# A four-layer hybrid trunk on one core: order of the start, width of v, place of o's transposes, and when norms and gates are issued

## The chip, the cores and the metric

One Trainium2 chip, of which the program uses one NeuronCore. The time is the device time of one execution in microseconds (us); the result compares medians of runs. The engines are PE (TensorE, matmuls and transposes by an identity), DVE (VectorE), ACT (ScalarE), POOL (GpSimd) and SP (SyncE, which here issues nearly all DMAs, one after the other in program order).

## The reference

The program computes four layers on x of 1024 positions by 1024 channels, all float32. Layers 0 and 3 are HGRN2, layer 1 is sliding-window attention, layer 2 is a gated DeltaNet:

```python
for i in range(4):
    shift, scale, gate = split(c @ ada_w[i] + ada_b[i], 3)      # 1024 each, from one vector c
    h = rmsnorm(x, norm_g[i]) * (1 + scale) + shift
    y = (hgrn2, swa, gdn)[i % 3](h, ...)                          # token mixer
    x = x + gate * y
# hgrn2: q, f, v, z = split(h @ w_in)  (8 heads of 128); per head a gated linear recurrence
#        S = f*S + k v^T, o = q S  (f = lb+(1-lb)*sigmoid(f_pre), k = (1-lb)*sigmoid(-f_pre))
#        y = (rmsnorm(o) * silu(z)) @ w_out
# swa:   16 query heads, 4 kv heads of 64, window 128, rotary angles from positions, sinks; gate silu(z)
# gdn:   q, k (8 heads), v, z (16 heads of 128), causal conv of 4 taps, silu, per-head decay,
#        delta rule with a triangular solve per chunk; y = (rmsnorm(o) * silu(z)) @ w_out
```

## The kernel before

**Precision and tiles.** Each float32 operand is split into a rounded high part and the rest, and each product is three matmuls (`mm3`, lines 204 to 206). Activations `hhi`, `hlo` lie with channels on partitions, in two halves of 512 positions (`hf` 0 and 1), 8 blocks (`k`) of 128 channels each. `load_w` (166) brings a weight tile of 256 KB by SP, ACT casts it to `w_hi` (179), DVE makes `w_lo` (180); four pairs are in flight. `proj_fm` gives 128 output channels by 512 positions (`proj_ps`, 24 matmuls of 512 columns per half). `proj_tm` (1170) gives positions by 256 channels (`projt_ps`, matmuls of 256 columns): v of HGRN for a pair of heads, and q, k, v of attention. `out_mm` (1204) is the output projection (`outp_ps`).

**Start.** `load_x` transposes x on PE and squares it on ACT. `ada_first` makes c @ ada_w in 512-wide parts, all four needed ones (2, 0, 3, 1, in that order, `AO`) as one-row matmuls on PE (400); `ada_cols` (449) turns a row into columns. Parts 2 and 0 hold the scale and shift of blocks 0 to 3, parts 3 and 1 those of blocks 4 to 7. `norm_apply` (496) conditions a half: per block one DVE product into `n_t`, one ACT instruction for `hhi` (505), one DVE instruction for `hlo` (506). The angle tables of attention (`rope_tables`) are made here too.

**Layers.** Each mixer is a generator. `weave` (68) steps several generators in the proportion of the costs that they yield: the mixing of unit or head n with the projections of n+1 and, as `side`, the ada matrices of the next layer on DVE (413). A list scheduler then orders the instructions of each engine by their place in the program, less the offset of `high_priority`; `early` (114) uses that for the first projections of a layer, and `tied` (138) holds a group of matmuls behind its first one.

**HGRN.** `mix` forms the causal products of each 128 positions by levels; the last (j = 32) takes three strips of 32 rows, of 96, 64 and 32 columns (1087). Then o per half (`o_ps`), its norm (1132), four transposes `ot_ps` (1136), the product with the gate z, and a store to the DRAM tile `od` by SP (1141), read back for the output projection. The last head stays on chip.

**DeltaNet.** `conv` copies a projection (644), scales it (648) and adds three shifted taps on DVE (650). `inverse` solves the triangular systems of a unit in small matmuls, the last of them four groups `z_ps`. `ZL` says in which unit the z of a later unit is projected, both halves (0, 1) at once mostly.

## Time and profile before

| | |
|---|---|
| median of 3 runs | 2692.0 us (2688.74 to 2692.27) |
| profiled execution | 2695.95 us, of which the span of the trace 2694.2 |
| PE busy | 2609.7 us, 97% of the span |
| DVE, ACT, POOL busy | 75%, 47%, 5% |
| layer 0, HGRN | 55 to 635 us |
| layer 3, HGRN | 2125 to 2694 us |

The profile is of one execution. "Busy" is the time in which an engine had an instruction at work; the wait rows give, for an engine's line, what it stood still for, the total, how often and the longest. PEclk is TensorE's granted clock as a share of full speed, in a window the mean over it.

### The profile page before, as it was taken

Reading aid. Unit: us, or ns where it says so; the run is one execution under the profiler, and the core shown is the slowest. Engines: PE = TensorE matmul, PEld = TensorE weight load, DVE = VectorE, ACT = ScalarE, POOL = GpSimd, SP = SyncE. Lnnn points to the kernel's source line nnn. Section 1 sums busy time; section 2 is a strip of 40 time slices with the busy share of each in tenths; the row PEclk is TensorE's granted clock in tenths of the full one; section 3 lists DMA queues with packets and bytes.
Section 4 is the critical chain, followed back from the end, with each engine's and each line's share of the span. In section 5 each row is a group of like instructions: output and inputs, shape, how many; then the busy total and the mean of one; then the engine's idle time right before and its main releaser. Section 6 shows DMA issues by size and latency. Waiting matters only on the chain.

```text
span 2694.2 us, 51458 instructions
## 1 busy us (share of the span) xinstructions
PE 2609.7 (97%) x18927; PEld 2102.4 (78%) x18927; DVE 2010.2 (75%) x5619; ACT 1272.9 (47%) x3268; POOL 136.7 (5%) x352
## 2 busy tenths in 40 slices
PE   8999999999999999999999999999999999999998
PEld 4878878778878777677877777777788878787877
DVE  6776766788687877777988888989876766656575
ACT  4333333444454655454556556666644433333342
POOL 0000100000000000001001101100000000000000
PEclk9999999999999999999999999999999999999999
DMA  6332222344223252333343333333584221111133
GB/s 241 92 93 84 68 79 72 110 137 157 59 87 103 75 158 91 114 98 84 102 115 99 96 105 100 94 97 82 179 254 132 71 60 37 56 51 43 49 118 115
DMA packets 361490, 273.29 MB, mean 101 GB/s; under 512 B 70499, under 2 KB 294166, under 8 KB 361238
## 3 DMA queue, kind: packets, MB, share of 16 engines
q1 hardware_dynamic: 360950, 268.96, 33.9%
q8 instruction: 149, 2.44, 0.4%
q14 instruction: 103, 0.84, 0.1%
q0 software_dynamic: 288, 1.05, 0.1%
HBM read 224.77 MB, written 45.15 MB: 100 GB/s over the span
## 4 chain that ended last, share of the span: by engine, by line
PE 71%; DVE 17%; DMA 5%; ACT 3%; issue 3%; SPq 1%; POOL 0%; DVEq 0%; ACTq 0%; POOLq 0%
PE proj_ps L206 10%; PE proj_ps L205 9%; PE proj_ps L204 9%; PE outp_ps L204 5%; PE outp_ps L205 5%; PE outp_ps L206 5%; DMA ada_w<-in_ada_w_dram 3%; PE projt_ps L204 3%; PE projt_ps L206 3%; PE projt_ps L205 3%; DVE w_lo L180 2%; DVE gd_tb L650 2%; PE pv_ps L1374 1%; DVE ada_acc L413 1%; PE w_ps L890 1%
## 5 line engine op out<-in xcount | busy, mean ns | idle before, releaser
L204 PE MATMUL proj_ps<-hhi,w_hi 128*128 128x512 f32 x1664 | 675.8, 406 | 6.1 <-ACT gd_tb L648 5.9
L206 PE MATMUL proj_ps<-hhi,w_lo 128*128 128x512 f32 x1664 | 679.9, 409 | 0.0
L205 PE MATMUL proj_ps<-hlo,w_hi 128*128 128x512 f32 x1664 | 671.2, 403 | 0.0
L204 PEld LDWEIGHTS proj_ps<-hhi,w_hi 128*128 128x128 f32 x1664 | 315.3, 190 | 59.4 <-ACT gd_tb L648 6.3
L205 PEld LDWEIGHTS proj_ps<-hlo,w_hi 128*128 128x128 f32 x1664 | 314.7, 189 | 59.0 <-issue 2.4
L206 PEld LDWEIGHTS proj_ps<-hhi,w_lo 128*128 128x128 f32 x1664 | 315.0, 189 | 56.1 <-issue 1.0
L179 ACT CAST w_hi<-w_raw 128x512 fp32r<-128x512 f32 x332 | 202.0, 611 | 303.3 <-PE proj_ps L205 188.1
L180 DVE TENSOR_TENSOR w_lo<-w_raw,w_hi 128x512 fp32r<-128x512 f32 x332 | 223.1, 674 | 155.2 <-ACT w_hi L179 129.1
L205 PE MATMUL projt_ps<-w_lo,hhi 128*128 128x256 f32 x896 | 258.7, 291 | 4.7 <-DVE w_lo L180 4.7
L204 PE MATMUL projt_ps<-w_hi,hhi 128*128 128x256 f32 x896 | 257.8, 290 | 0.6 <-ACT w_hi L179 0.6
L206 PE MATMUL projt_ps<-w_hi,hlo 128*128 128x256 f32 x896 | 256.8, 290 | 0.0
L204 PE MATMUL outp_ps<-o_hi,w_hi 128*128 128x512 f32 x576 | 229.2, 400 | 4.7 <-ACT o_hi L1200 3.4
L205 PE MATMUL outp_ps<-o_lo,w_hi 128*128 128x512 f32 x576 | 229.4, 399 | 0.0
L206 PE MATMUL outp_ps<-o_hi,w_lo 128*128 128x512 f32 x576 | 226.8, 396 | 0.7 <-DVE w_lo L183 0.7
L205 PEld LDWEIGHTS projt_ps<-w_lo,hhi 128*128 128x128 f32 x896 | 171.1, 192 | 8.1 <-DVE w_lo L180 6.0
L204 PEld LDWEIGHTS projt_ps<-w_hi,hhi 128*128 128x128 f32 x896 | 171.1, 192 | 3.7 <-ACT w_hi L179 1.0
L206 PEld LDWEIGHTS projt_ps<-w_hi,hlo 128*128 128x128 f32 x896 | 170.8, 192 | 2.4 <-issue 1.0
L650 DVE SCALAR_TENSOR_TENSOR gd_tb<-gd_xs,taps,gd_tb 128x512 f32<-128x512 f32 x192 | 145.2, 756 | 28.3 <-ACT gd_tb L648 19.7
L182 ACT ACTIVATE w_hi<-w_raw,par 128x512 fp32r<-128x512 f32 (+1 forms) x136 | 94.3, 698 | 137.0 <-PE outp_ps L205 89.2
L204 PEld LDWEIGHTS outp_ps<-o_hi,w_hi 128*128 128x128 f32 x576 | 108.8, 189 | 29.1 <-ACT o_hi L1200 4.9
L413 DVE SCALAR_TENSOR_TENSOR ada_acc<-ada_w,par,ada_acc 128x512 f32<-128x512 f32 x140 | 104.8, 749 | 33.4 <-DMA ada_w<-in_ada_w_dram 32.5
L206 PEld LDWEIGHTS outp_ps<-o_hi,w_lo 128*128 128x128 f32 x576 | 108.7, 189 | 23.5 <-DVE w_lo L183 1.3
(398 smaller groups left out, 4894.8 us busy)
## 6 DMA issues: line engine op xcount, KB each, us to landing
ada_w<-in_ada_w_dram SPq DMA_DIRECT2D x160, 256.0 KB, 2.8
w_raw<-in_hg_in_w_dram SPq DMA_DIRECT2D x136, 256.0 KB, 2.8
w_raw<-in_gd_in_w_dram SPq DMA_DIRECT2D x108, 256.0 KB, 3.0
o_in<-od SPq DMA_DIRECT2D x72, 256.0 KB, 3.2
w_raw<-in_gd_out_w_dram SPq DMA_DIRECT2D x64, 256.0 KB, 2.9
w_raw<-in_sw_in_w_dram SPq DMA_DIRECT2D x48, 256.0 KB, 2.9
w_raw<-in_hg_out_w_dram SPq DMA_DIRECT2D x40, 256.0 KB, 2.8
ada_w<-in_ada_w_dram SPq DMA_DIRECT2D x8, 1024.0 KB, 9.2
```

The costliest lines, as they stand in the source:

```text
L179: nc.scalar.copy(hi, raw)
L180: nc.vector.tensor_tensor(lo, raw, hi.bitcast(F32), ALU.subtract)
L182: nc.scalar.activation(hi, raw, AF.Copy, scale=scale)
L204: mm(out, a[0], b[0], start=start, stop=False)
L205: mm(out, a[0], b[1], start=False, stop=False)
L206: mm(out, a[1], b[0], start=False, stop=stop)
L413: self.nc.vector.scalar_tensor_tensor(acc, w, c, acc, ALU.mult, ALU.add)
L650: nc.vector.scalar_tensor_tensor(y, xs[:, j:j + HT], w(j), y, ALU.mult, ALU.add)
L890: nc.tensor.matmul(po[:, hd[a]], dd["u"][a, hf][:, cs], rhs, start=True, stop=True)
L1374: nc.tensor.matmul(po[a * 64:(a + 1) * 64], vg[:, n + 1 - nkb + b, :], p4[:, :, a, :], start=b == 0, stop=b == nkb - 1)
```

## The change

- **Start.** x's first half is fetched first and transposed, then ada parts 2 and 0 and two weight tiles each. `norm_apply` is a generator now: blocks 0 to 3 are made after parts 2 and 0, blocks 4 to 7 after parts 3 (PE) and 1 (DVE). x's later half comes after all of this; its transposes use the PSUM banks `tr` and `s`. The first projections get their places before the conditioning of the later half (`k.start`). The angle tables are made by the side stream of layer 0.
- **v of HGRN.** `load_wide` and `proj_wide` replace `proj_tm`: 512 channels at a time, four heads, evacuated into the slots of x, which is spilled to DRAM and filled again before the output projection. Spills and fills go by POOL's queue, those of layer 0's start by SP's.
- **o of HGRN, heads 0 to 6.** DVE writes the normed o in an order of 32-wide blocks, transposes it in 32 by 32 squares, and four DMAs store it into the DRAM tile `pd`; `gate()`, called at the third level of the next half, loads it, multiplies it by z, stores it to `od`.
- **Last level.** Four strips of 64, 64, 32 and 32 columns in place of three; the diagonal copies by ACT.
- **Norm's later half.** Before layer 2 its blocks are taken four at a time from within `conv` (`self.last`, `parts`, `hold`), and z of units 1 and 2 is projected early; `n_t` lies in PSUM. Before the other layers it is drained at the start of the mixer.
- **DeltaNet.** The four `z_ps` groups are held behind the last projection matmul (`apart`) and yield 2200; z of units 1 to 5 is projected by halves in two units.
- **Attention.** v and q first, k later, with one rsqrt per two blocks; the four pv matmuls in one group. Output: x is written from `hslot` tiles.

```diff
-NS = 8, 16, 10
...
-ZL = ((2, 0, 1),), ((3, 0, 1),), ((4, 0, 1),), ((5, 0, 1),), ((6, 0),), ((6, 1),), ((7, 0, 1),), ()
...
+ZL = ((2, 1), (3, 0)), ((3, 1), (4, 0)), ((4, 1), (5, 0)), ((5, 1),), ((6, 0),), ((6, 1),), ((7, 0, 1),), ()
...
+    def apart(self, mms):
+        with self.tc.issue_after(self.mm.ins):
+            self.tied(mms)
...
+    def load_wide(self, w, c0, pool):
+        return [self.load_w(w[:, k, c0:c0 + HT], None, (None, pool)[k % 2]) for k in range(KT)]
...
+                pt = self.psum(("tr", "s")[g], "x_ps", 1) if hf else self.proj_ps("x_ps")
...
+        for c in range(NC):
+            nc.scalar.activation(sq, xts[c], AF.Square, accum_out=ssq[:, c:c + 1])
...
+    def ada_load(self, i, part):
...
+        wk = self.hslot("ada_w0").bitcast(F32)
+        for g in range(2):
+            self.nc.sync.dma_start(wk[:, 4 * g:4 * g + 4, :], w[:, 4 * g:4 * g + 4, part * HT:(part + 1) * HT])
+        return wk
...
+    def ada_first(self, i, part, acc, wk, bank):
...
+        if bank:
+            pr = self.psum(*bank)
+            for k in range(KT):
+                nc.tensor.matmul(pr[0:1, :], self.cT[:, k:k + 1], wk[:, k, :], start=k == 0, stop=k == KT - 1)
...
+                self.ada_step(acc, wk[:, k, :], k)
+        self.ada_cols(i, part, acc)
...
-            t = self.np.tile([P, HT], F32, name="n_t", tag="n_t", bufs=NB["n_t"])
+            t = self.psum("lev", "n_t", 2)
...
-            nc.scalar.activation(hhi[:, k, :], t, AF.Identity, bias=S)
+            self.piece = nc.scalar.activation(hhi[:, k, :], t, AF.Identity, bias=S)
...
+            yield 1
...
-            nc.scalar.copy(xs[:, 3:], ps)
+            with self.tc.issue_after(self.hold.ins) if self.hold else nullcontext():
+                nc.scalar.copy(xs[:, 3:], ps)
...
-                nc.vector.scalar_tensor_tensor(y, xs[:, j:j + HT], w(j), y, ALU.mult, ALU.add)
...
+                last = nc.vector.scalar_tensor_tensor(y, xs[:, j:j + HT], w(j), y, ALU.mult, ALU.add)
+            self.piece = None
+            with self.tc.issue_after(last.ins):
+                drain(take(self.last, self.parts))
+            self.hold = self.piece
...
-            with self.burst():
...
+            self.apart([lambda g=g, z=z, p_=p_, b_=b_: nc.tensor.matmul(z[R[b_], g, :], uv[R[p_], g, R[b_]], Tc[R[p_], g, :], start=True, stop=True)
+                        for g in range(N) for z, p_, b_ in ((za, 0, 1), (zb, 2, 3))])
...
-            yield 900
+            yield 2200
...
-        self.early(proj_kq(0, ds[0], ((0,),)), EV)
+        self.parts = 4
+        self.early(chain(proj_kq(0, ds[0], ((0,),)), proj_z(1, ds[1], (0,)), proj_z(2, ds[2], (0,))), EV)
+        drain(self.last)
...
-        weave(self.tc, (inverse(0, ds[0]), 28000, 0, 0.8, 100),
-              (chain(proj_z(0, ds[0], (1,)), proj_v(0, ds[0]), proj_z(1, ds[1]), proj_kq(1, ds[1])), 72800, 0, 1, 0))
+        weave(self.tc, (inverse(0, ds[0]), 34300, 0, 0.85, 100),
+              (chain(proj_z(0, ds[0], (1,)), proj_v(0, ds[0]), proj_z(1, ds[1], (1,)), proj_kq(1, ds[1])), 62400, 0, 1, 0))
...
-            ws = self.load_tm(w_in, 2 * D + 2 * m * P)
...
+        def proj_v(m):
...
+            def ev(tt, ps):
+                hf, c = divmod(tt, NC)
+                if vs[hf] is None:
+                    vs[hf] = self.xslot("hg_v").rearrange("p (c a) n -> p c (a n)", a=2)
...
+                nc.scalar.copy(vs[hf][:, c, m * HT:m * HT + n], ps[:, :n])
...
+            yield from self.proj_wide(self.load_wide(w_in, 2 * D + m * HT, mp), ev, range(2 * NC))
...
+        def gate():
...
+            h, hf, z = pend.pop()
+            rows = (slice(h * P, (h + 1) * P), slice(hf * HT, (hf + 1) * HT))
+            t = tl("tmp")
+            nc.sync.dma_start(t, self.pd[rows])
+            nc.vector.tensor_tensor(v4(z, "c b"), v4(t, "b c"), v4(z, "c b"), ALU.mult)
+            nc.sync.dma_start(od[rows], z)
...
-                            nc.gpsimd.tensor_copy(at[gs, :, gs], A[gs].rearrange("p (c t) -> p c t", c=NC))
+                            nc.scalar.copy(at[gs, :, gs], A[gs].rearrange("p (c t) -> p c t", c=NC))
...
+                        def mm(c, k, g, x, b):
+                            return nc.tensor.matmul(pl[g * 32:(g + 1) * 32, c, b], kg[:, c * P + k * 32:c * P + (k + 1) * 32], xv[:, c, x, :], start=True, stop=True)
+                        self.tied([lambda c=c, m=m: mm(c, *m) for c in range(NC) for m in (
+                            (0, 3, slice(6, 7), slice(3, 4)), (0, 0, slice(0, 4, 3), slice(1, 3)),
+                            (1, 1, slice(1, 5, 3), slice(2, 4)), (2, 2, slice(2, 3), slice(3, 4)))])
+                        for k, g, b0, b1 in ((0, 0, 1, 3), (1, 1, 2, 4), (2, 2, 3, 4), (0, 3, 3, 4)):
+                            nc.scalar.copy(at[k * 32:(k + 1) * 32, :, b0 * 32:b1 * 32], pl[g * 32:(g + 1) * 32, :, b0:b1, :].rearrange("p c b t -> p c (b t)"))
                         yield 900
+                    if l == 3 and pend:
+                        gate()
...
-                nc.vector.tensor_tensor(on.rearrange("p (c t) -> p c t", c=NC), po.rearrange("p (c t) -> p c t", c=NC), r[:, :, None].to_broadcast([P, NC, P]), ALU.mult)
-                pt = self.psum("tr", "ot_ps", 1)
...
-                    nc.tensor.transpose(pt[:, cs], on[:, cs], self.ident)
...
-                nc.vector.tensor_tensor(of, pt, d["zs", hf], ALU.mult)
                 if h < HA:
-                    nc.sync.dma_start(od[h * P:(h + 1) * P, hf * HT:(hf + 1) * HT], of)
...
+                    nc.vector.tensor_tensor(v4(on, "b c"), v4(po, "c b"), r[:, :, None, None].to_broadcast([P, NC, 4, 32]), ALU.mult)
+                    ob = tl("tmp")
+                    nc.vector.transpose(ob, on)
+                    dst = self.pd[h * P:(h + 1) * P, hf * HT:(hf + 1) * HT].rearrange("(b q) (a t) -> a q b t", b=4, a=4)
+                    for a in range(4):
+                        nc.sync.dma_start(dst[a], ob[a * 32:(a + 1) * 32].rearrange("q (b t) -> q b t", b=4))
+                    pend.append((h, hf, d["zs", hf]))
...
+        drain(self.last)
...
-        self.early(chain(proj(0, ds[0], "qf", (0,)), take(gv, 8)))
+        if i == 0:
+            for g, at, n in ((proj(0, ds[0], "qf", (0,)), self.start[0], 80), (take(gv, 16), self.start[1], 0)):
+                self.early(g, eo=self.tc.cur_priority - at + n)
+            rst = ExitStack()
+            rp = rst.enter_context(self.tc.tile_pool(name="rope", bufs=1, reuse_waits="tile"))
+            side = chain(take(side, 18), self.rope_tables(rp), side)
+        else:
+            self.early(chain(proj(0, ds[0], "qf", (0,)), take(gv, 16)))
+        self.spill_x(1, None if i else nc.sync)
...
+            rst.close()
+        for hf in range(2):
+            self.fill_x(hf)
...
+    def proj_wide(self, ws, evac, tts):
+        for tt in tts:
+            ps = self.proj_ps("projw_ps")
+            hf, ts = tt // 4, slice((tt % 4) * P, (tt % 4 + 1) * P)
+            for k in range(KT):
+                self.mm3(ps, (self.hhi[hf][:, k, ts], self.hlo[hf][:, k, ts]), ws[k], k == 0, k == KT - 1)
+                if k % 2:
+                    yield 1300
+            evac(tt, ps)
...
+                self.tied([lambda b=b, a=a: nc.tensor.matmul(po[a * 64:(a + 1) * 64], vg[:, n + 1 - nkb + b, :], p4s[b][:, :, a, :], start=b == nkb - 1, stop=b == 0)
+                           for b in reversed(range(nkb)) for a in range(2)])
+                yield 860 * nkb
...
+        def proj_v(hf):
+            return self.proj_tm(self.load_tm(w_in, 1280), ev_v, (2 * hf, 2 * hf + 1))
...
+        self.early(chain(proj_v(0), proj_q(0, ds[0], (0, 1))))
...
+        drain(self.proj_tm(self.load_tm(w_in, 1024), ev_k))
+        drain(chain(proj_z(0, ds[0]), proj_q(0, ds[0], (2, 3))))
...
+        ada = []
+        for part, bank, col in ((2, ("lev", "ada_row", 2), 0), (0, ("lev", "ada_row", 2), D), (3, ("s", "ada_row", 1), None), (1, None, None)):
+            acc = sp.tile([P, HT], F32, name="ada_acc", tag="acc", bufs=3)
+            ada.append((layers[0], part, acc, k.ada_load(layers[0], part), bank))
+            if layers[0] == 0 and col is not None:
+                k.preload(hg_in_w[0], (col,))
+        rb = k.norm_stats(0, k.load_x(sp, 0, x0, sq))
+        a = k.norm_apply(layers[0], 0, rb)
+        for n in range(2):
+            for x in ada[2 * n:2 * n + 2]:
+                k.ada_first(*x)
+            drain(take(a, KT // 2))
+        drain(a)
+        k.start = [tc.cur_priority]
+        k.fetch_x(1, x1)
+        ssq = k.load_x(sp, 1, x1, sq)
+        k.spill_x(0, tc.nc.sync)
+        rb = k.norm_stats(1, ssq)
+        k.start.append(tc.cur_priority)
+        drain(k.norm_apply(layers[0], 1, rb))
...
+                a = k.norm_apply(nxt, hf, k.norm_stats(hf))
+                if hf == 0:
+                    drain(a)
                     k.spill_x(0)
-                if hf == 1:
+                else:
+                    k.last = a
```

**PE at the program's start**, before: the tail of the ada rows (par is c as columns, `ada_w_362` and `_383` are the third and fourth part), x's later half and the first projection.

```order
L400 MATMUL ada_row<-ada_w_362,par 1x512 x7
L400 MATMUL ada_row<-ada_w_383,par 1x512
L449 MATMUL ada_ps<-ones,ada_acc 128x1 x4
L400 MATMUL ada_row<-ada_w_383,par 1x512 x7
L310 MATMUL x_ps<-ident,x_in 128x128 x9
L449 MATMUL ada_ps<-ones,ada_acc 128x1 x4
L310 MATMUL x_ps<-ident,x_in 128x128 x23
L265 MATMUL taps_ps<-ident,taps_in 128x128
L204 MATMUL proj_ps<-hhi,w_hi 128x512
L205 MATMUL proj_ps<-hlo,w_hi 128x512
```

After, from the third PE row of the program on:

```order
L321 MATMUL x_ps<-ident,x_in 128x128 x32
L423 MATMUL ada_row<-ada_w_150,par 1x512 x3
L513 MATMUL n_rb<-n_sq,ones 128x512
L423 MATMUL ada_row<-ada_w_150,par 1x512 x5
L423 MATMUL ada_row<-ada_w_166,par 1x512
L472 MATMUL ada_ps<-ones,ada_acc 128x1 x4
L423 MATMUL ada_row<-ada_w_166,par 1x512 x7
L472 MATMUL ada_ps<-ones,ada_acc 128x1 x4
L423 MATMUL ada_row<-ada_w_182,par 1x512 x3
L213 MATMUL proj_ps<-hhi,w_hi 128x512 x2
L214 MATMUL proj_ps<-hlo,w_hi 128x512
```

The transposes of x's first half stand ahead of all ada rows, and the first projection stands behind the first three matmuls of the third part instead of behind all four parts and x's later half.

**ACT at the start of layer 2 (DeltaNet)**, before: `hhi` are the blocks of the later half, `gd_xs` the first convolution's copy.

```order
L179 CAST w_hi<-w_raw 128x512
L505 ACTIVATE hhi<-n_t,mod 128x512
L179 CAST w_hi<-w_raw 128x512
L505 ACTIVATE hhi<-n_t,mod 128x512 x2
L179 CAST w_hi<-w_raw 128x512
L505 ACTIVATE hhi<-n_t,mod 128x512 x2
L644 COPY gd_xs<-proj_ps 128x512
L648 ACTIVATE gd_tb<-proj_ps,taps 128x512
L644 COPY gd_xs<-proj_ps 128x512
```

After, at the same place:

```order
L184 CAST w_hi<-w_raw 128x512 x3
L667 COPY gd_xs<-proj_ps 128x512
L671 ACTIVATE gd_tb<-proj_ps,taps 128x512
L577 CAST gd_wab<-w_raw 128x8x32
L184 CAST w_hi<-w_raw 128x512
L614 ACTIVATE gd_tmp<-gd_tmp 128x16
L679 ACTIVATE gd_tb<-gd_tb 128x512
L184 CAST w_hi<-w_raw 128x512
L526 ACTIVATE hhi<-n_t,mod 128x512 x2
L706 COPY gd_kt<-ktr_ps 128x512
L693 ACTIVATE gd_tb,gd_ms<-ktr_ps 128x128 x4
L184 CAST w_hi<-w_raw 128x512
```

The copy of the convolution stands ahead of the blocks of the later half, which come two by two behind the work of the convolution.

**SP in the first HGRN layer, around the first head's store**, before (`ada_w` are the side stream's loads, `w_raw` weights):

```order
L177 DMA w_raw<-in_hg_in_w_dram 128x4x128 x2
L427 DMA ada_w<-in_ada_w_dram 128x512 x3
L1141 DMA od_76<-hg_tmp 128x512
L427 DMA ada_w<-in_ada_w_dram 128x512 x2
L177 DMA w_raw<-in_hg_in_w_dram 128x4x128 x2
L427 DMA ada_w<-in_ada_w_dram 128x512 x3
```

After:

```order
L182 DMA w_raw<-in_hg_in_w_dram 128x4x128 x2
L450 DMA ada_w<-in_ada_w_dram 128x512
L1190 DMA pd<-hg_tmp 32x4x128 x4
L450 DMA ada_w<-in_ada_w_dram 128x512 x3
L1069 DMA hg_tmp<-pd 128x512
L450 DMA ada_w<-in_ada_w_dram 128x512
L182 DMA w_raw<-in_hg_in_w_dram 128x4x128 x2
L1071 DMA od_76<-hg_zs 128x512
L450 DMA ada_w<-in_ada_w_dram 128x512 x3
L182 DMA w_raw<-in_hg_in_w_dram 128x4x128 x3
```

One store of o has become four stores into `pd`, a load from it and a store to `od`, with weight loads between and behind them.

## Rows read from the trace of the kernel before

**Rows 1.** Totals of the page: busy us, share of the span, instructions.

```profile
PE 2609.7 (97%) x18927; PEld 2102.4 (78%) x18927; DVE 2010.2 (75%) x5619; ACT 1272.9 (47%) x3268; POOL 136.7 (5%) x352
```

**Rows 2.** Windows: stretch, length, busy us (instructions) of PE, PEld, DVE, ACT, POOL; PEclk, DMA share, GB/s.

```profile
0.00:55.10 55.10, 45.84 (x166) 18.89 (x166) 29.93 (x108) 23.24 (x41) 3.91 (x43) 0.97 0.80 285
55.00:635.00 580.00, 562.49 (x4754) 462.16 (x4753) 415.33 (x1206) 218.45 (x492) 33.02 (x71) 0.99 0.31 93
1131.00:1150.00 19.00, 13.03 (x50) 8.40 (x49) 13.17 (x20) 9.81 (x26) 2.92 (x10) 0.82 0.28 71
1250.00:1900.00 650.00, 636.88 (x4483) 510.37 (x4473) 566.36 (x1632) 399.13 (x1273) 53.98 (x135) 0.99 0.37 96
2125.00:2694.00 569.00, 554.65 (x4756) 459.12 (x4754) 358.48 (x1102) 206.43 (x468) 29.37 (x64) 1.00 0.21 64
```

**Rows 3.** Start: PE's order of time (start, length, what), then the DMA's GB/s, 0 to 70 us in 40 slices.

```profile
14.41 3.11 PE L400 MATMUL ada_row<-ada_w,par 128*1 128x512 f32 x4 [1.28 <-DMA ada_w<-in_ada_w_dram]
55.11 0.50 PE L204 MATMUL proj_ps<-hhi,w_hi 128*128 128x512 f32 x1
GB/s 0 22 143 365 402 61 365 423 393 386 392 385 375 305 330 397 420 241 268 386 404 382 383 372 385 410 227 21 0 140 197 0 0 5 111 48 144 6 51 114
```

**Rows 4.** PE's groups by form: busy us, mean ns, idle before with its cause.

```profile
L400 PE MATMUL ada_row<-ada_w,par 128*1 128x512 f32 x64 | 29.7, 613 | 1.3 <-DMA ada_w<-in_ada_w_dram 1.3
L1136 PE MATMUL ot_ps<-ident,hg_tmp 128*128 128x128 f32 x128 | 20.8, 280 | 5.9 <-DVE hg_tmp L1132 5.6
L1087 PE MATMUL lev_ps<-hg_X,hg_kg 128*32 128x96 f32 x256 | 27.1, 249 | 0.0
L1087 PE MATMUL lev_ps<-hg_X,hg_kg 128*32 128x64 f32 x256 | 20.9, 224 | 0.0
```

**Rows 5.** Windows of outp_ps (512 columns), then projt_ps (256), back to back; PE first.

```profile
2000.00:2050.00 50.00, 50.00 (x223) 41.39 (x222) 6.72 (x9) 1.00 0.72 224
699.00:706.00 7.00, 7.00 (x60) 7.00 (x60) 1.34 (x3) 1.19 (x2) 1.00 0.01 2
```

**Rows 6.** Windows of projt_ps, then proj_ps, over layer 3.

```profile
2125.00:2694.00 569.00, 105.21 (x768) 96.27 (x768) 0.00 (x0) 9.39 (x16) 1.00 0.21 64
2125.00:2694.00 569.00, 292.25 (x1138) 204.34 (x1136) 22.00 (x32) 36.26 (x64) 1.00 0.21 64
```

**Rows 7.** PE's waits: line <- what it waited for: us, times, longest.

```profile
PE z_ps L828 <- DVE gd_uq L823: 6.6, 7, 1.6
PE proj_ps L204 <- ACT gd_tb L648: 5.9, 1, 5.9
PE ot_ps L1136 <- DVE hg_tmp L1132: 5.6, 11, 1.3
PE projt_ps L205 <- DVE w_lo L180: 4.7, 5, 1.4
PE ab_ps L575 <- DVE gd_tb L727: 2.0, 1, 2.0
```

**Rows 8.** ACT in order of time at the start of layer 2.

```profile
1134.82 1.38 ACT L505 ACTIVATE hhi<-n_t,mod 128x512 fp32r<-128x512 f32 x2 [1.07 <-DVE n_t L504]
1136.10 0.57 ACT L644 COPY gd_xs<-proj_ps 128x512 f32<-128x512 f32 x1
```

**Rows 9.** Groups of ACT and DVE: busy us, mean ns, idle before.

```profile
L179 ACT CAST w_hi<-w_raw 128x512 fp32r<-128x512 f32 x332 | 202.0, 611 | 303.3 <-PE proj_ps L205 188.1
L180 DVE TENSOR_TENSOR w_lo<-w_raw,w_hi 128x512 fp32r<-128x512 f32 x332 | 223.1, 674 | 155.2 <-ACT w_hi L179 129.1
L413 DVE SCALAR_TENSOR_TENSOR ada_acc<-ada_w,par,ada_acc 128x512 f32<-128x512 f32 x140 | 104.8, 749 | 33.4 <-DMA ada_w<-in_ada_w_dram 32.5
L859 DVE STREAM_TRANSPOSE gd_of<-gd_of 128x512 f32<-128x512 f32 x32 | 22.5, 704 | 0.1
```

**Rows 10.** SP's queue: its longest wait; then a store from the chain.

```profile
SPq L177 <- DVE w_lo L180: 570.3, 153, 27.3
1235.95 2.00 DMA tblk<-gd_Tb
```

More of the change, by code (lines that the diff above doesn't have):

```diff
@@ L100, in __init__ @@
         self.x = [None, None]
-        self.oo, self.pre = {}, {}
+        self.oo, self.pre, self.last, self.parts = {}, {}, iter(()), 0
+        self.piece = self.hold = None
     def hslot(self, name):
@@ new lines, in rope_tables @@
+            tab = self.rope[-1].rearrange("p (w a b) -> p w a b", w=2, a=8)
+            for w, src in enumerate((cs, ang)):
+                for a in range(2):
+                    gg = gb[:, a if w == 0 else 1 - a, :][:, None, :].to_broadcast([P, 8, 32])
+                    t = tmp("cg")
+                    if w == 1 and a == 0:
+                        nc.vector.scalar_tensor_tensor(t, src, -1.0, gg, ALU.mult, ALU.mult)
+                    else:
+                        nc.vector.tensor_tensor(t, src, gg, ALU.mult)
+                    nc.gpsimd.dma_start(tab[:, w, :, a * 32:a * 32 + 32], t)
+                yield 1
@@ L833, in inverse @@
             nc.vector.tensor_copy(Z[up, 8:16], z[lo])
-            yield 900
+            yield 2200
             z = bank("z_ps", 64)
-            self.tied([lambda g=g, q=q: nc.tensor.matmul(z[q, g % 8, :], Z[up, g, :], uv[up, g, up], start=True, stop=True)
+            self.apart([lambda g=g, q=q: nc.tensor.matmul(z[q, g % 8, :], Z[up, g, :], uv[up, g, up], start=True, stop=True)
                        for n in range(8) for g, q in ((n + 8, up), (n, lo))])
```

268 lines of the change are left out of this document (118 added, 150 removed).

## The prediction, made before the changed kernel was run

> **What bounds the kernel now.** I read the engine totals first. TensorE (PE) is busy 97% of the span [rows 1], so only work taken off PE, or a wait of PE removed, moves the end. The windows come next [rows 2]. The first 55.1 us hold 45.8 us of PE time without one projection. The two HGRN layers (55 to 635, 2125 to 2694) keep PE at 97% with VectorE (DVE) at 72% and 63%. The DeltaNet stage (1250 to 1900) has PE at 98% and DVE at 87%: DVE is the second limit there. Third, the start in order of time [rows 3]: the first small matmul on ada weights is at 14.41, the first projection at 55.11, and the DMA moves about 385 GB/s up to 46 us. Fourth, PE's own waits [rows 7], and the start of DeltaNet on ScalarE (ACT) [rows 8].
>
> The profiled execution took 2695.95 us, its span 2694.2 and 1.75 around it. Its span is the base of the sum, and the result is carried to the median of 2692.0, which lies 4 us lower.
>
> **The start.** Before, the 48 matmuls of q and f for half 0 begin at 55.11. At the steady spacing 50/223 = 0.224 us [rows 5] they end at 66. After, x's first half, ada parts 2 and 0 and four weight tiles, 7.3 MB, come first: at 385 GB/s from 3 us on they are there at 22. PE needs about 7.4 us per part (29.7 us over four parts [rows 4]). The second MB of part 0 lands near 21, its four matmuls end near 25, and with the column matmuls and one block's conditioning the first projection starts near 28. A block is two DVE instructions of the L413 kind, 2 × 0.749 = 1.5 us [rows 9], beside one on ACT; four follow one another, so the first 24 matmuls end near 34. Blocks 4 to 7 need parts 3 and 1 (11.5 MB, 33 us). Part 1 now runs on DVE: 8 steps of the same kind, 6 us, with two weight splits and two blocks between, to about 42. On ACT the four squares of x's later half stand ahead of block 4, and its last tile lands near 40. So blocks 4 to 7 run from 42 to 48, and q and f end near 49: 17 us earlier. Against that, PE has little to do between 36 and 42. In 1131 to 1150, where PE stood still for 6 us, the clock fell to a mean of 0.82 [rows 2]. At the lower of its two levels, 1.2 GHz in place of 2.4, 24 matmuls cost 24 × 0.224 = 5.4 us more. I take −14 (−19 to +2). The 4 MB of spills that layer 0 adds come after 40 us, where the DMA was nearly idle.
>
> **v of the HGRN layers by 512 columns.** Per layer 768 matmuls of 256 columns become 384 of 512. Steady spacings are 7/60 = 0.117 and 0.224 us [rows 5]: 89.6 against 86.1. In the layer itself projt_ps took 105.2 for 768 and proj_ps 292.25/1138 = 0.257 each [rows 6]: 384 of these are 98.6. The ends are 105.2 − 86.1 = 19 gained and 98.6 − 89.6 = 9 lost per layer. I take both rates from the same layer: 6.6 each, −13 for two (−38 to +18). The number of weight tiles and splits is unchanged.
>
> The Trainium skill (TensorE: Matmul & The Clock Gate, section Back-to-back issue gap) gives 262 cycles for 256 columns and 518 for 512, so halving the matmuls would gain about 1 us per layer by my estimate. The trace's steady spacings are both some 7% above that and agree with its proportion; the layer's do not.
>
> **Transposes of o.** 112 of the 128 ot_ps transposes leave PE: 20.8 × 112/128 = 18 us, and PE waited 5.6 us for their input [rows 4, 7]. Instead DVE transposes (0.704 [rows 9]) and multiplies by the gate later: two instructions for one, about 0.7 × 28 = 20 us over both layers, where DVE idles 375 us [rows 2]. On the path: −16 (−23 to −8), since some of that time overlapped neighbours.
>
> **The last level of HGRN.** Per 128 positions three 32-row strips of 96, 64 and 32 columns become four of 64, 64, 32 and 32. A 96-wide one takes 249 ns on average, a 64-wide one 224 [rows 4], but there is one more. −4 (−9 to +9). The diagonal copies move from GpSimd to ACT, 38% busy there [rows 2]: nothing on the path.
>
> **DeltaNet's start.** ACT copies the first convolution input at 1136.10, behind all eight blocks of the later half [rows 8]; PE waits 5.9 us for it, then 2.0 for the later half [rows 7]. Now the blocks stand behind the convolutions, and z of units 1 and 2 fills PE meanwhile. With part of the low clock: −9 (−11 to 0).
>
> **The z groups of the inverse** are tied behind a projection matmul and yield more. PE waits 6.6 us before the third group [rows 7]; between the groups still stand 6 to 8 matmuls, so I take −3 (−7 to 0).
>
> **Attention.** The k blocks wait for weights at the layer's head, 4.7 us [rows 7]; v and q now go first, and k's norm runs once per two blocks. The pv matmuls run in one group instead of two. −7 (−10 to 0).
>
> **Output** without its own pool: −1.
>
> **Added.** z of units 1 to 5 is loaded once per half: 20 more casts (0.611) and splits (0.674 [rows 9]), 13.5 us of DVE where it is 87% busy. The cover is the remaining 13%; without it all 13.5 count. +4 (0 to 13.5). The HGRN layers spill x and fill it again on GpSimd's queue; the fill of the first half has half a head's time before it is used. The new round trip of o at the last heads sits before the output projection. Together +3 (0 to 12). The angle tables, some 10 us of DVE, move from the start into layer 0, where DVE has room: 0.
>
> Sum: −14 −13 −16 −4 −3 −9 −7 −1 +4 +3 = −60. Span 2634, profiled run 2636, median 2632.
>
> **Rivals.** *The load queue stalls the weights (slower).* SyncE issues in order. In each of 28 head halves it now waits for four stores to pd to land before it reads them back, and for the gate multiply before it stores. A store of this kind lands in 2.00 us [rows 10]; with the multiply a round is some 5 us, 140 in all, and what is queued behind are weight loads. For it: nothing else brings weights. Against it: SyncE spent 570 us waiting for a free weight buffer [rows 10], so it runs ahead; four pairs of tiles are 96 matmuls, 22 us of PE. It decides where that wait for a buffer falls below 5 us. If half of it comes through, +70: 2702.
>
> *DVE becomes the limit in DeltaNet.* Then the 20 splits count in full and the z groups gain nothing: +9.5 +3 = 2645. For it: 87%. Against it: PE's waits for DVE there are mostly below 2 us.
>
> *Columns set the pace.* v gains only the difference of the steady spacings, 89.6 − 86.1 = 3.5 per layer, instead of 6.6: 2632 + 6 = 2638. For it: per column the two spacings differ by 4% only. Against it: the layer's own rate of 0.137 per 256 columns (105.2/768). By that rule of the Trainium skill it would be 2643.
>
> *The start stays bound by DMA and the low clock:* no 14 us: 2646. For it: 385 GB/s to 46 us. Against it: blocks 0 to 3 need only half of those bytes.
>
> *The far ends hold* for the start, v and the transposes: −19, −38, −23, 37 more than the sum: 2595.
>
> *The change only swaps waits:* every queue is reordered, and new waits of PE eat the gain: 2690.
>
> **Numbers.** My sum 0.30; columns 0.17; DVE 0.15; start 0.14; far ends 0.14; queue 0.06; swapped waits 0.04. Columns, DVE and start at once would give 6 + 13 + 14 = 33 more, 2665, and are inside these chances. Range 2598 to 2676: it leaves out the queue, the swap and part of the far ends. Faster by more than 0.2% (about what a measurement of this kernel can tell) is all but the last two: 0.90; within 0.2%: 0.04; slower: 0.06.
>
> **What would show it.** The start: first projection near 28 us, q and f of half 0 ended near 49; wrong if the first comes after 40. v: 384 projw_ps in under 100 us per HGRN layer. ot_ps down to 16 matmuls and no wait of 1 us for it. No 5.9 us wait for gd_tb at DeltaNet's head, and the clock above 0.95 there. PE's waits for z_ps below 4 us. DVE in DeltaNet below 92%. SyncE's wait on pd short, and no w_hi or w_lo among PE's longest waits in the HGRN layers; if they are there, the forecast is wrong.

## The result and the profile after

The changed kernel takes 2701.82 us (median of 5 runs, 2694.15 to 2704.30), the kernel before 2692.27 in the same comparison: a ratio of 1.0033, interval 1.0021 to 1.0046. It is 0.33% slower, where 2632 was forecast. The profiled execution took 2704.3 us, its span 2702.6. Its totals, against [rows 1]:

```profile
PE 2588.0 (96%) x18287; PEld 2057.6 (76%) x18287; DVE 2017.1 (75%) x5647; ACT 1323.2 (49%) x3468; POOL 95.6 (4%) x244
```

PE has 22 us less work and the span is 8 longer, so PE idles 30 us more; the mean granted clock fell from 0.992 to 0.985. Work came off PE as planned, and waits took its place.

The table cuts each trace at the first matmul of the next stage (us; "out" is the part from a layer's first `outp_ps` to the next layer's first projection, for layer 3 to the last matmul). The last three columns are experiments told below. Each column is one profiled execution, and a stage varies between them: the DeltaNet layer took 803.7 to 814.8 us in the traces of e5, e11, e12, e13 and e14, where its code is the same. So a difference of under some 10 us in that stage is not told by one pair of traces.

| stage | before | after | e1: SP queue | e5: and DeltaNet as before | e16: and n_t in SBUF |
|---|---|---|---|---|---|
| start | 55.1 | 34.4 | 33.9 | 34.2 | 34.2 |
| layer 0 (HGRN) | 471.4 | 477.1 | 475.2 | 475.2 | 477.8 |
| layer 0 out | 104.9 | 113.0 | 110.5 | 110.2 | 104.8 |
| layer 1 (attention) | 353.9 | 353.9 | 346.3 | 346.4 | 346.4 |
| layer 1 out | 126.7 | 140.0 | 133.3 | 134.6 | 131.2 |
| layer 2 (DeltaNet) | 817.9 | 828.1 | 827.8 | 808.3 | 801.2 |
| layer 2 out | 190.4 | 190.6 | 190.5 | 190.0 | 189.4 |
| layer 3 (HGRN) | 461.9 | 454.1 | 451.9 | 451.8 | 450.5 |
| layer 3 out | 106.3 | 105.5 | 105.5 | 106.4 | 105.5 |

From before to after, the start and layer 3 gain 29 us; layer 0, its output, that of layer 1 and DeltaNet lose 37.

**Where it was lost beside the output projections.** Beside that of layer 1, POOL issues the spill of x's first half; then the DMA issues of 1038.5 to 1042 (size, median us to landing), and ACT, DVE and PE in order of time:

```profile
1038.24 0.89 POOL L127 DMA_DIRECT2D xd<-x  x1 [92.78 <-DVE x L556]
```

```profile
xd<-x POOLq DMA_DIRECT2D x1, 2048.0 KB, 8.5
w_raw<-in_sw_out_w_dram SPq DMA_DIRECT2D x2, 256.0 KB, 6.7
```

```profile
1047.06 0.92 ACT L184 CAST w_hi<-w_raw 128x512 fp32r<-128x512 f32 x2 [3.72 <-DMA w_raw<-in_sw_out_w_dram]
```

```profile
1047.71 0.69 DVE L185 TENSOR_TENSOR w_lo<-w_raw,w_hi 128x512 fp32r<-128x512 f32 x1 [3.59 <-ACT w_hi L184]
```

```profile
1049.86 2.07 PE L513 MATMUL n_rb<-n_sq,ones 128*128 128x512 f32 x2 [3.61 <-DVE n_sq L511]
```

This is read from the bottom up. PE waits 3.61 us for a tile of the norm, which needs no weight. DVE makes it late, since the split of a weight stands ahead of it; that waits for ACT's cast, and the cast for a load that took 6.7 us, where weight loads take 2.8 to 3.4 in the median (the page's lines on DMA issues). PE stops in the same way at 571, 952 and 1914 us, each time 8 us behind a transfer by POOL, with a load of `w_raw`, `ada_w` or `gd_tmp` at the end of the chain. (At 1914 the wait row of ACT's copy names `o_in`; but the copy reads `gd_tmp`, whose loads landed just then, at 1917.7.) Behind such a stop the clock is low for some microseconds. Windows at two of them (the last columns are clock, DMA share, GB/s):

```profile
570.00:580.00 10.00, 5.74 (x22) 4.67 (x21) 4.85 (x11) 3.49 (x6) 0.00 (x0) 0.74 0.55 153
1050.00:1060.00 10.00, 10.00 (x32) 7.17 (x33) 6.88 (x11) 3.59 (x7) 0.00 (x0) 0.70 0.18 50
```

The first holds the stop itself; the second begins right behind the stop of 3.61 us, and in it PE is busy all the time, at a mean of 0.70 of full speed.

**The start.** PE in order of time, then SP's issues, then two windows:

```profile
34.35 0.72 PE L213 MATMUL proj_ps<-hhi,w_hi 128*128 128x512 f32 x2
41.21 3.59 PE L423 MATMUL ada_row<-ada_w,par 128*1 128x512 f32 x8
53.38 1.86 PE L472 MATMUL ada_ps<-ones,ada_acc 128*128 128x1 f32 x8 [1.22 <-DVE ada_acc L436]
63.44 0.39 PE L215 MATMUL proj_ps<-hhi,w_lo 128*128 128x512 f32 x1
```

```profile
29.49 0.63 SPq L307 DMA_DIRECT2D x_in<-in_x_dram  x1
41.36 0.33 SPq L182 DMA_DIRECT2D w_raw<-in_hg_in_w_dram  x1
42.89 0.90 SPq L307 DMA_DIRECT2D x_in<-in_x_dram  x2
```

```profile
34.40:63.80 29.40, 25.96 (x103) 17.08 (x103) 17.90 (x38) 13.22 (x23) 0.99 (x2) 0.83 0.56 199
50.00:60.00 10.00, 8.10 (x29) 6.23 (x28) 7.72 (x17) 5.68 (x11) 0.99 (x2) 0.53 0.48 186
```

The first projection is at 34.35, against 55.11 [rows 3]. But the 48th ends near 64, where it ended near 67 before. The first projections now stand ahead of the last half of part 3's rows (41.21). On DVE the addition to the columns of part 3 waits for PE until 46.7:

```profile
46.71 0.16 DVE L474 TENSOR_TENSOR mod<-ada_ps,adab 128x4 f32<-128x4 f32 x1 [4.23 <-PE ada_ps L472]
```

All steps of part 1 but the first stand behind it in DVE's order, and part 1 is done only at 53. SP waits from 30 to 41 us for a free weight tile, with three tiles of x's later half behind it.

**HGRN.** Layer 3's `projw_ps` in a window of its own, then groups of the whole trace, against [rows 4, 6]:

```profile
2137.00:2591.00 454.00, 98.51 (x384) 70.46 (x384) 9.86 (x24) 1.00 0.26 79
```

```profile
L1197 PE MATMUL ot_ps<-ident,hg_tmp 128*128 128x128 f32 x16 | 2.5, 281 | 0.3 <-DVE hg_tmp L1193 0.2
L1133 PE MATMUL lev_ps<-hg_X,hg_kg 128*32 128x64 f32 x512 | 20.5, 222 | 0.0
L1133 PE MATMUL lev_ps<-hg_X,hg_kg 128*32 128x32 f32 x512 | 16.5, 200 | 1.4 <-DVE hg_F L1144 1.2 <-DVE hg_X L1111 0.2
```

v took 98.5 us, the forecast 98.6; 112 transposes and their wait are gone, and the level's strips sum to 37.0 us of busy time, where the two wider forms alone took 27.1 + 20.9 us before [rows 4]. Busy times of neighbours overlap, so this isn't what the level gives; e13 prices it.

### The profile page after: what moved, and what is told of

Same layout as the page of the kernel before. It is cut to its first block, busy times and chain, and to the rows that moved or that the text cites. A ratio compares the mean times of both kernels' runs of the same rounds, so it can differ in the third digit from the quotient of the medians.

```text
span 2702.6 us, 50547 instructions
## 1 busy us (share of the span) xinstructions
PE 2588.0 (96%) x18287; PEld 2057.6 (76%) x18287; DVE 2017.1 (75%) x5647; ACT 1323.2 (49%) x3468; POOL 95.6 (4%) x244
## 4 chain that ended last, share of the span: by engine, by line
PE 55%; issue 20%; DVE 14%; DMA 6%; ACT 3%; SPq 1%; POOL 0%; DVEq 0%; ACTq 0%; POOLq 0%
PE proj_ps L215 8%; PE proj_ps L213 8%; PE proj_ps L214 8%; PE outp_ps L213 4%; PE outp_ps L214 4%; PE outp_ps L215 4%; PE projw_ps L214 2%; PE projw_ps L215 2%; DVE gd_tb L673 2%; PE projw_ps L213 2%; DMA ada_w<-in_ada_w_dram 1%; DVE w_lo L185 1%; PE w_ps L916 1%; PE w_ps L932 1%; PE s_ps L1170 1%
## 5 line engine op out<-in xcount | busy, mean ns | idle before, releaser
L184 ACT CAST w_hi<-w_raw 128x512 fp32r<-128x512 f32 x352 | 214.2, 612 | 295.3 <-PE proj_ps L214 148.6
L185 DVE TENSOR_TENSOR w_lo<-w_raw,w_hi 128x512 fp32r<-128x512 f32 x352 | 236.2, 675 | 147.0 <-ACT w_hi L184 142.6
L436 DVE SCALAR_TENSOR_TENSOR ada_acc<-ada_w,par,ada_acc 128x512 f32<-128x512 f32 x147 | 109.7, 746 | 34.9 <-DMA ada_w<-in_ada_w_dram 34.2
L188 DVE SCALAR_TENSOR_TENSOR w_lo<-w_raw,par,w_hi 128x512 fp32r<-128x512 f32 (+1 forms) x136 | 97.0, 715 | 50.4 <-ACT w_hi L187 49.0
L213 PEld LDWEIGHTS outp_ps<-o_hi,w_hi 128*128 128x128 f32 x576 | 110.5, 192 | 30.9 <-ACT o_hi L1285 8.7
L214 PEld LDWEIGHTS outp_ps<-o_lo,w_hi 128*128 128x128 f32 x576 | 110.9, 193 | 24.3 <-DVE o_lo L1286 1.8
L214 PE MATMUL projt_ps<-w_lo,hhi 128*128 128x256 f32 x384 | 110.6, 290 | 2.3 <-DVE w_lo L185 2.3
L215 PE MATMUL projt_ps<-w_hi,hlo 128*128 128x256 f32 x384 | 110.7, 290 | 0.0
L213 PE MATMUL projt_ps<-w_hi,hhi 128*128 128x256 f32 x384 | 110.5, 290 | 0.2 <-ACT w_hi L184 0.2
L214 PE MATMUL projw_ps<-w_lo,hhi 128*128 128x512 f32 x256 | 103.2, 404 | 1.8 <-DVE w_lo L185 1.8
```

Source lines behind the costliest of these rows:

```text
L184: nc.scalar.copy(hi, raw)
L185: nc.vector.tensor_tensor(lo, raw, hi.bitcast(F32), ALU.subtract)
L188: nc.vector.scalar_tensor_tensor(lo, raw, scale, hi.bitcast(F32), ALU.mult, ALU.subtract)
L213: mm(out, a[0], b[0], start=start, stop=False)
L214: mm(out, a[0], b[1], start=False, stop=False)
L215: self.mm = mm(out, a[1], b[0], start=False, stop=stop)
```

## The experiments

All times are medians against the kernel before on the same chip. A ratio's interval is some ±0.0013, 3.5 us; a difference between two kernels is taken from their ratios, times 2691, and below some 5 us it isn't told from nothing. In the diffs "..." marks what is left out. Line numbers are those of each kernel's own page.

**e1.** The transfers of x back on SP's queue.

```diff
-        (queue or self.nc.gpsimd).dma_start(self.xd..., self.x[hf])
+        (queue or self.nc.sync).dma_start(self.xd..., self.x[hf])
...
-        self.nc.gpsimd.dma_start(self.x[hf], self.xd...)
+        self.nc.sync.dma_start(self.x[hf], self.xd...)
```

> After, with the twelve spills and fills of x that go by POOL's queue put back on SP's. Theory A (a 2 MB transfer on its own queue takes the 16 DMA engines for 8.7 to 9.9 us just when weights are due; a weight load beside it takes 8 us in place of 2.8, and the cast that waits for it holds ACT's other work up): the five stalls of PE at 571, 626, 952, 1046 and 1914 us (4.4 + 1.3 + 3.3 + 3.8 + 4.4 = 17 us) go, and with the low clock behind them some 20 to 28 us: 2674 to 2682. Rival B (2 MB hold the DMA engines whichever queue they come from; what was lost lies elsewhere): 2697 to 2707.

2681.87 us, ratio 0.9962 (0.9949 to 0.9976): 19 us faster than the changed kernel, theory A's size. (There are fourteen such transfers; the expectation says twelve.)

**e2.** The kernel before with its eight transfers on POOL's queue (the same edit the other way).

> Before, with its eight spills and fills of x moved from SP's queue to POOL's, nothing else. Theory A: the stalls of 3 to 4 us appear here too, at four of the eight transfers, 15 to 25 us in all with the clock: 2707 to 2717. Rival B: 2689 to 2696.

2707.32 us, 1.0063 (1.0051 to 1.0075): 17 us slower than before by the queue alone. So the choice of queue is shown as the cause of 17 to 19 us. Theory A's picture of a slow load does not tell the queues apart, since on SP's queue the weight loads issued behind a transfer are late too. These are the issues at the same spill in the kernel before:

```profile
xd<-x SPq DMA_DIRECT2D x1, 2048.0 KB, 8.0
w_raw<-in_sw_out_w_dram SPq DMA_DIRECT2D x2, 256.0 KB, 7.8
```

What differs is the order of other work. Both kernels have the same number of instructions on PE, DVE and ACT, but in e2 some of ACT's and DVE's stand in another order behind the transfer. Here are the squares of the norm (`n_sq`), the cast of a weight (`w_hi`) and PE's next step of the norm (`n_ps`) beside layer 0's output projection, in e2 and then in the kernel before:

```profile
579.94 0.63 ACT L482 ACTIVATE n_sq<-x 128x512 f32<-128x512 f32 x1 [0.63 <-DVE n_acc L483]
586.23 0.72 ACT L182 ACTIVATE w_hi<-w_raw,par 128x512 fp32r<-128x512 f32 x1 [5.66 <-DMA w_raw<-in_hg_out_w_dram]
586.86 0.61 ACT L482 ACTIVATE n_sq<-x 128x512 f32<-128x512 f32 x1
589.62 1.84 PE L486 MATMUL n_ps<-ones,n_acc 128*128 128x1 f32 x8 [4.19 <-DVE n_acc L483]
```

```profile
581.41 0.63 ACT L482 ACTIVATE n_sq<-x 128x512 f32<-128x512 f32 x1 [0.63 <-DVE n_acc L483]
585.69 1.84 ACT L182 ACTIVATE w_hi<-w_raw,par 128x512 fp32r<-128x512 f32 x3
583.22 0.95 PE L486 MATMUL n_ps<-ones,n_acc 128*128 128x1 f32 x8
```

Before, all squares stand ahead of the casts, and a late load holds nobody up. In e2 a cast stands between the squares, waits 5.66 us for its load, and the norm waits with it. PE stops so behind the transfers at 577, 1050 and 1122 us, for 4.19, 3.17 and 1.98 us. A fourth stop, of 3.81 us behind the fill at 1901, has another way: small loads of `gd_tmp`, which stood ahead of the fill on SP's queue before, now run beside it. Their issues before, then in e2:

```profile
gd_tmp<-tblk SPq DMA_DIRECT2D x8, 32.0 KB, 2.2
```

```profile
gd_tmp<-tblk SPq DMA_DIRECT2D x5, 32.0 KB, 9.1
```

The four stops sum to 13 of the 17 us; before, PE waits less than 0.5 us at the same steps. The changed kernel and e1 differ in these two ways at 571, 952, 1046 and 1914. That the order alone, on one queue, costs this was not tried by itself.

By the Trainium skill (Trainium Kernel Development and Optimization, section Key Constraints) the queues of SP, ACT and POOL share the same 16 DMA engines, and issuing from several of them saves only issue time. By that rule alone e1 and e2 would have changed nothing; the runs differ from it by 17 to 19 us, and the rows above put most of that down to what was reordered with the queue.

**e3.** v by 256 channels in tiles of its own; x is then neither spilled nor filled in the HGRN layers.

```diff
-            yield from self.proj_wide(self.load_wide(w_in, 2 * D + m * HT, mp), ev, range(2 * NC))
...
+            ws = self.load_tm(w_in, 2 * D + 2 * m * P)
...
+                yield from self.proj_tm(ws, ev, (2 * hf, 2 * hf + 1))
...
-            self.fill_x(hf)
```

> After, with v of the HGRN layers projected 256 channels at a time into tiles of its own as before, and so without the eight transfers of x that these layers had gained. The prediction's term: 13 us slower, 2715. Rival C (the pace is set by the columns, 3.5 us a layer, and the transfers are hidden): 2707 to 2710. Rival D (the eight added transfers and the wider tiles cost more than v gains): 2685 to 2700.

2704.36 us, 1.0054 (1.0042 to 1.0067): 3 us slower than the changed kernel by the medians, 6 by the ratios, so between rivals D and C and far from the prediction's 13. e11 repeats it without POOL's queue.

**e4.** The 112 transposes back on PE, without the round trip through pd.

```diff
+                    nc.tensor.transpose(pt[:, cs], on[:, cs], self.ident)
...
-                    nc.vector.transpose(ob, on)
...
-                        nc.sync.dma_start(dst[a], ob[a * 32:(a + 1) * 32]...)
...
+                    nc.sync.dma_start(od[h * P:(h + 1) * P, hf * HT:(hf + 1) * HT], of)
```

> After, with the 112 transposes of o back on PE and one store of o, without the round trip through pd and the late gate. The prediction's term: 16 us slower, 2718. Rival E (a transpose costs its own spacing of 0.107 us, 12 us in all, and the wait stays away): 2712 to 2714. Rival F (the round trip and SP's waits for it eat what PE gains): 2695 to 2704.

2722.32 us, 1.0119 (1.0105 to 1.0132): 23 us slower. The transposes on DVE are worth more than forecast. SP's waits in the changed kernel for pd to land, and for the multiply ahead of the store, are short (us in total, times, longest):

```profile
SPq L1069 <- DMA pd<-hg_tmp: 18.9, 20, 2.6
SPq L1071 <- DVE hg_zs L1070: 37.0, 19, 4.3
```

**e5.** On e1: the whole DeltaNet layer as before.

```diff
-        self.parts = 4
-        self.early(chain(proj_kq(0, ds[0], ((0,),)), proj_z(1, ds[1], (0,)), proj_z(2, ds[2], (0,))), EV)
         drain(self.last)
+        self.early(proj_kq(0, ds[0], ((0,),)), EV)
```

(and `ZL`, the groups and their yields as in the kernel before)

> The base is the changed kernel with x's transfers on SP's queue (2682 us). Here the whole DeltaNet layer is as before: the later half conditioned ahead of the convolutions, z of units 1 to 5 both halves at once, the z groups tied as before. The prediction's terms (9 + 3 gained, 4 lost) would make it 8 slower: 2690. My reading of the base's trace (this layer takes 828 us up to its output projection, before 818, with equal work and 11 us more of stalls on PE): 10 faster, 2672.

2662.42 us, 0.9899 (0.9886 to 0.9912): 17 us faster than e1, more than I had read from the trace. The layer takes 808 us, 10 less than before; that 10 is from one trace each, and traces of this layer vary as much. What is left of the change in it is n_t in PSUM, and that the later half's blocks are emitted inside the layer's function, behind its setup and nearer to its first projections. ACT copies the first convolution input ahead of a block (L526), where before the copy stood behind all eight [rows 8]:

```profile
1107.74 0.59 ACT L667 COPY gd_xs<-proj_ps 128x512 f32<-128x512 f32 x1 [2.29 <-PE proj_ps L215]
1112.52 0.69 ACT L526 ACTIVATE hhi<-n_t,mod 128x512 fp32r<-128x512 f32 x1 [1.19 <-DVE n_t L525]
```

PE's wait of 5.9 us for `gd_tb` [rows 7] is 0.2 here, and in the layer's first 140 us PE idles 3.4 us, where it idled 10.2 before. So I put the gain down to the later emission; it was not tried by itself.

**e6, e9, e10, e15: which part of DeltaNet.** e6 is e1 with only the groups as before. e9 is e5 with z early and by halves; e10 is e5 with only the pieces (`self.parts = 4`); e15 is e6 without the hold:

```diff
-            with self.tc.issue_after(self.hold.ins) if self.hold else nullcontext():
+            with nullcontext():
                 nc.scalar.copy(xs[:, 3:], ps)
```

> The same base; only the four groups of small matmuls of the inverse are tied and weighted as before (yields 900 to 1300), z stays early and by halves. The prediction's term: 3 slower, 2685. If the groups, not the early z, brought the layer's new stalls (w_ps 6 us more, transposes 3 more): 2672 to 2676. If they are neutral: 2680 to 2684.

> The base is now the changed kernel with x's transfers on SP's queue and the DeltaNet layer as before (2662 us). Added back: z of units 1 and 2 early and z of units 1 to 5 by halves (20 more weight tiles); the groups and the conditioning stay as in the base. The prediction priced these at +4 (0 to 13.5). If the second loading is what costs (20 casts and splits, 13.5 us of DVE in a layer where DVE is 86% busy): 2674 to 2680. If the conditioning by pieces is what costs: 2660 to 2667.

> The same base of 2662; added back only the conditioning of the later half in pieces of four blocks from within the convolutions, each next convolution held behind them, without early z. If the pieces cost: 2672 to 2680. If early z and its halves cost: 2658 to 2665. With the prediction's term (9 gained at the layer's start, of which the base has its part already): 2655 to 2660.

> The kernel with early z, halves and pieces (2677.5 us, groups as before), without the hold that keeps the next convolution's copy behind the pieces. If the hold makes the pieces and the early z collide: 2660 to 2668. If it is the pieces' place on ACT and DVE ahead of the weight splits of the early z: 2674 to 2680.

e6: 2677.55 us, 0.9959 (0.9946 to 0.9971); e9: 2666.04, 0.9912 (0.9898 to 0.9926); e10: 2659.05, 0.9889 (0.9873 to 0.9905); e15: 2677.44, 0.9951 (0.9938 to 0.9964). The groups are neutral. Early z alone costs 3.5 us and the pieces alone gain 3 (on e16's base they cost 5, e17): neither is told from nothing. Both together (e6 against e5) cost 16. The hold (each next convolution issued only behind the pieces) is not the reason. PE's longest wait in the first 41 us of the layer, in e15, then in e9:

```profile
PE proj_ps L215 <- DVE w_lo L185: 6.3, 2, 4.1
```

```profile
PE n_rb L513 <- DVE n_sq L511: 0.4, 1, 0.4
```

With the pieces, PE stands still for the low parts of weights; without them it doesn't. It idles 7.7 us of these 41 in e15 and 0.7 in e9, which is most of the 10 us between the two kernels. In program order the pieces stand ahead of the early z, so DVE makes them ahead of the splits that early z waits for. That this order is the reason was not tried by itself.

**e7.** On e1: pv as before, each pair of matmuls behind its own block (the `tied` group taken out).

> The same base; only pv of attention is as before, each pair of matmuls behind its own block. The base gains 7.6 us in this layer up to its output projection and loses 6.6 us beside it. If the tied group brings the loss at the tail (nothing is left there to fill its wait): 2675 to 2678, the stage beside the output projection near 127 us. If the transfers and the conditioning bring it: 2680 to 2686.

2680.51 us, 0.9963 (0.9950 to 0.9976): neutral. The layer's head grew by 4 us and the stage beside the output projection shrank by 1.5.

**e8, e12.** The start as before, on e1 and on e5: all ada rows on PE, the angle tables and x's later half ahead of the first projection.

> The same base; the program's start is as before: all ada rows on PE, the angle tables and x's later half ahead of the first projection, at 55 us. The prediction's term: 14 slower, 2696. My reading of the trace (the first 48 projection matmuls end at 63 us, before at 67; 13 us that the start had done stand in layer 0 now): 4 to 8 slower, 2686 to 2690. If the moved work costs layer 0 as much as the start gave: 2680 to 2684.

> The same base of 2662; the start as before, which in the run before this one made no difference (2679 against 2682). If that holds here: 2657 to 2664, the fastest kernel so far. If the new start was hidden there behind something that this base has lost: 2668 to 2676.

2679.34 us, 0.9961 (0.9950 to 0.9973), and 2662.54, 0.9901 (0.9887 to 0.9914). Both stand within 1 us of their base by the ratios. In e12 the first projection is at 55.0 and layer 0's output projection begins at 506.4; in e5 34.2 and 509.4. The new start gives nothing: what it leaves out stands in layer 0.

**e11.** On e5: v as in e3.

> The same base of 2662; v of the HGRN layers by 256 channels as before, without the eight transfers of x that the wide v needs. The prediction's terms (13 gained, some 3 lost): 2672 to 2675. By the steady spacings alone (3.5 us a layer): 2669. If the transfers take the gain back on SP's queue too: 2658 to 2665.

2666.59 us, 0.9912 (0.9897 to 0.9928): 3.5 us slower, not told from nothing; layer 3 alone takes 457.2 us in place of 451.8. That falls between two of the three prices: the columns alone (2669) and transfers that take the gain back (2658 to 2665); the prediction's 13 is farther off.

**e13.** On e5: the last level as before (three strips, diagonal copies by POOL).

> The base of 2662 (x's transfers on SP's queue, DeltaNet as before); the last level of HGRN as before: three strips of 96, 64 and 32 columns, the diagonal copies on GpSimd. The prediction's term: 4 slower, 2666. If the fourth strip, and four copies more on ACT ahead of the output of a half, cost what layer 3 misses (10 + 5 expected from transposes and v, 10 seen, in two layers): 2652 to 2657. If neither: 2660 to 2664.

2671.47 us, 0.9921 (0.9908 to 0.9934): 6 us slower; my suspicion was wrong and the new level is worth its term. In the traces the two HGRN layers took 14 us more in all (482.4 for 475.2, 458.5 for 451.8) and the DeltaNet layer, which the edit doesn't touch, 5 less.

**e14.** On e5: the whole attention layer as before.

> The base of 2662; the whole attention layer as before (k with v first, k's norm per block, pv per block). The prediction's term: 7 slower, 2669, with the stage beside the output projection still near 134 us. If the layer's own edits bring the loss beside the output projection: 2661 to 2664, that stage back near 127 us and the head of the layer 7 us longer.

2674.61 us, 0.9944 (0.9930 to 0.9957): 12 us slower; in the traces the layer itself takes 358.3 us against 346.4. The stage beside the output projection stays at 133.8: its loss against 126.7 comes from something that all these kernels share.

**e16, e17.** On e5 and on e10: `n_t` of a layer's first half in SBUF.

```diff
-            t = self.psum("lev", "n_t", 2)
+            t = self.psum("lev", "n_t", 2) if hf else self.np.tile([P, HT], F32, name="n_t", tag="n_sq", bufs=NB["n_sq"])
```

> The base of 2662; n_t of the first half of each layer in SBUF (two tiles shared with the norm's squares), no longer in the PSUM banks that the last head's levels use. If the shared banks cost what the stages beside the output projections of layers 0 and 1 lost: 2650 to 2655, these stages at 105 and 127 us. If the loss comes from x's transfers and the order of the weight loads there: 2659 to 2665, the stages still 110 and 134 us.

> The same with the pieces of the later half in DeltaNet (2659 without the edit). Shared banks: 2646 to 2652, the fastest kernel. Otherwise 2656 to 2662.

2650.29 us, 0.9858 (0.9842 to 0.9875): 11 us faster than e5 and the fastest kernel here; e17 2657.29, 0.9875 (0.9861 to 0.9890). The stage beside layer 0's output projection, in e5 and in e16:

```profile
509.40:619.60 110.20, 104.67 (x571) 82.72 (x572) 83.58 (x172) 49.97 (x97) 2.44 (x5) 0.94 0.43 134
```

```profile
512.10:616.80 104.70, 100.36 (x442) 78.90 (x443) 78.48 (x147) 46.69 (x86) 1.90 (x5) 0.98 0.46 143
```

With n_t in the two `lev` banks, 129 more PE instructions fall into this stage, 128 of them the small `lev_ps` matmuls of the last head, and the clock falls to 0.94: the last head's levels need the same banks and slip behind the norm. In SBUF the stage is as before (104.9), while layer 0 ahead of it grows by 2.6. The stage of layer 1 came back by 3 of 8 us. DeltaNet took 7 less, which is within what traces of the same layer vary: PE was busy 788.4 us on the same 5446 instructions in e5 and 781.0 in e16, at clocks of 0.99 and 1.00. So where the rest of the 11 us lies is not shown.

## Why the prediction was wrong

**The chain of loss.** Each row is a step as the prediction put it, with what the runs measured.

| step | forecast | measured | by |
|---|---|---|---|
| start | −14 | 0 | e8, e12 |
| v by 512, with its transfers | −13, +3 | −3.5 to −6 | e11, e3 |
| transposes of o | −16 | −23 | e4 |
| last level | −4 | −6 | e13 |
| attention | −7 | −12 | e14 |
| DeltaNet's start, z groups, z halves | −9, −3, +4 | −10 by the later emission, +17 by the rest (groups 0) | e5, e6 |
| transfers by POOL's queue | none; the HGRN layers' own in +3 | +17 to +19 | e2, e1 |
| n_t in PSUM | no term | +11 | e16 |

From the changed kernel to e16 three losses were taken out one after the other: the queue (19 us), DeltaNet's edits other than the later emission (17) and n_t's banks (11), 47 in all. What is open lies in the gains. The edits that e16 keeps were forecast at −61 together; the prices measured for them sum to −55 to −64, and e16 gained 38. So some 16 to 26 us are not explained by single edits (the −10 of the later emission was measured with n_t in PSUM and overlaps the +11). The gains were priced on different bases and, as early z and the pieces show, edits don't add; which other pairs collide stays open.

**The step that failed most** is "Added", in two ways. It priced the fills by who waits for the fill ("half a head's time before it is used"), gave the move to another queue no term of its own, and spoke only of HGRN. The edit moved all transfers of x, those of layers 1 and 2 too, and with them the order of ACT's and DVE's other work. Nobody waits for the spill; PE waits for a norm tile behind a split behind a cast behind a load. That is 17 to 19 us (e1, e2). And n_t's new place, which is in the diff, got no term at all: 11 us (e16).

**DeltaNet's start** seems right in its mechanism: with the blocks behind the convolution's copy the 5.9 us wait goes, and the layer takes 10 less in e5's trace (forecast 9). The step "z of units 1 and 2 fills PE meanwhile" failed: the filling work has weights of its own, whose splits stand on DVE behind the blocks that it was to hide; early z and the pieces together cost 16 (e6 against e5).

**The start** failed at "Part 1 now runs on DVE … to about 42" and "its last tile lands near 40". Both took each engine's own time and left out what stands ahead in its queue: DVE's addition to part 3's columns, which waits for PE, and SP's wait for a free weight tile. Part 1 came to 53, and the last tile was issued at 43 and landed near 50, in a stretch at clock 0.53, near the lower of TensorE's two levels. The condition "wrong if the first comes after 40" looked at the wrong event: it came at 34 and nothing was gained, because the last of the 48 ended near 64, where 49 was forecast.

**v**: I took the layer's own rates for both widths. The wide rate held to 0.1 us (98.5). The gain did not: e3 and e11 give 3.5 to 6 for both layers together, where I expected 13. Of the prediction's own two prices that of the columns (7 for two layers) is nearer. The prediction's sentence that both steady spacings are "some 7%" above the cycles it cites is right for 256 columns alone; that of 512 columns is 4% above, so their proportion agrees only roughly.

**The rivals.** The load queue's rival gave 2702, the measured time, by a cause that was not at work: SyncE's waits for pd and for the multiply sum to 56 us where it had 140, PE's longest wait for a weight tile in the two HGRN stages was 1.0 us, and without the round trip the kernel is slower (e4). "The change only swaps waits" (2690, chance 0.04) comes nearest in kind. I gave both little, because the waits visible before summed to little; a reordered queue makes new ones.

**The base of the chances** failed too: eight gains were summed at their own price, as if they added. The queue's stops lie beside output projections or in the last 40 us ahead of them, and the loss by early z with the pieces in a layer's first 41 us. There 3 to 4 us of waiting come with a lower clock; what that adds was not measured by itself.
